# Second products of an expert step moved between the halves of the next step's up products

## The chip, the cores and the metric

One core of a Trainium2 chip runs the whole program. The metric is device time in microseconds, the median of several runs; lower is better. The profile and the trace come from one execution of their own.

## The reference, cut to what matters

The program is a two-layer encoder trunk over 272 tokens (256 and 16 meta tokens) of width 1024. The part that matters here is the channel mixer of the second layer: a router sends each token to two of eight experts, and each expert is a SwiGLU of width 3584.

```python
def swiglu(h, w_gate, w_up, w_down):
    return (jax.nn.silu(h @ w_gate) * (h @ w_up)) @ w_down

for e in range(N_EXPERTS):
    y = y + combine[..., e:e + 1] * swiglu(h, e_gate[e], e_up[e], e_down[e])
```

All weights are float32: 8 experts x 3 x 1024 x 3584, read once from HBM.

## The kernel before, in words

The experts are ordered by the number of their tokens. The five fullest are "big" (room for 128 rows), the last three "small" (room for 64). Each expert's width of 3584 is cut into seven slices of 512, so that there are 56 steps, 35 big and 21 small. `steps` is their order, fixed when the program is built: the first seven are big, then a small step stands behind every big one or every second one, and the last four are big.

A step has three products. The gate product `pg` and the up product `pu` (`project`, L1148) multiply the step's rows, as the stationary operand, with 512 columns of weights, over eight blocks `k` of 128 features. The second product, or down product (`down`, L1220), multiplies the flipped result of the step, `hh` and `hl` (`hs` for small ones), with 8 blocks of weights into `pyb0`, `pyb1` (or `pys0`, `pys1`), which add up over an expert's seven steps. The flip is done by transposes on TensorE and evictions (`flip_later`, L1190, big; `flip_small`, L1199, small; the latter also adds the two halves and applies the SiLU, in three further pieces of work that are put into `side`).

The order is written out by hand: in step i come the gate products (the flip of step i - 1 ahead of block k = 4), the up products, then the down products of step i - 1. Engines run their own instructions in this order.

A weight comes as a tile of 128 x 2048 float32 (`raw`, 1024 KB), loaded by SP's queue (L84); 15 such tiles fit. It has two units of 1024 columns, two blocks each. To be multiplied with float32's precision at a faster rate, a unit is split in two: ScalarE casts the high part `w_hi` (L104), VectorE subtracts to get the low part `w_lo` (L127). Four units are held in this split form (`W_BUFS`). Big rows are split as well, so a block takes three matmuls (high x high, high x low, low x high, L1159, L1163, L1165); small rows have high and low side by side in the 128 columns of the stationary operand, so a block takes two. One unit in four of the gate and up weights of a big step is "plain": it is multiplied as it is, in full float32, and needs no split.

`W.release` gives a unit back and issues the next cast, `W.lo` issues the subtraction, and `beside` (L1135) does both with one piece of `side` between them, after every second block. When both units of a tile are split or used, the next tile is loaded into its place. `keep_rows` (L1095) takes the sums of a finished expert to `y_rows` in HBM by ScalarE's queue; `fetched` brings the rows of the next expert by transposes in four pieces (`behind`).

Of the kernel before, what the change touches and what calls it, by code (L numbers as in the profile page):

```python
# [39 lines left out]
ALONE, IDS_AT, COUNT_AT, SUMS_FROM, QUIET = 6, 1, 2, 4, 3  # L40
PLAIN_AT = 6
BIG, CAP, SMALL_CAP = 5, 128, 64
LAST_AHEAD, LAST_FLIP, LAST_TABLE = 3, 3, (0, 2)
POOL_AFTER = (2, 4, 6, 7)

# [120 lines left out]
def body(tc, xT, w_pw1, w_pw2, w_gu, w_dn, w_pool, m_gate, m_up, m_down, small, moe_g,  # L166
# [34 lines left out]
    tiles = []  # L201
# [17 lines left out]
    steps = [(of_small if i in small_at else of_big).pop(0) for i in range(NE * FT)]  # L219
    expert_at = {}  # L220

    def tile_of(w, q, f, p):
        return w[expert_at[q], f, p] if q else w[0, f, p]

    def moe_tile(w, i):
        q, f = steps[i]
        for p in range(2):
            plain = (1,) if q < BIG and p and w is not m_down else ()
            tiles.append((lambda p=p: tile_of(w, q, f, p), [1024, 1024], plain))

    for i in range(len(steps)):
        moe_tile(m_gate, i)
        moe_tile(m_up, i)
        if i:
            moe_tile(m_down, i - 1)
    moe_tile(m_down, len(steps) - 1)
    W = Weights(nc, raw_pool, hi_pool, lo_pool, tiles)
    load_x(0)
    W.load(parts=[(256, lambda k=k: load_x(k)) for k in (2, 4, 6)] +
# [85 lines left out]
    def blocks(w, n):  # L325
        return [t.rearrange("p (k m) -> p k m", k=n) for t in w]
# [25 lines left out]
    def add_mean(ps, n, x):  # L352
        PE.matmul(ps, lhsT=mean, rhs=x, start=(n == 0), stop=(n == KC - 1))


    with ExitStack() as cs:
# [131 lines left out]
        def sums(lag=0):  # L488
            ready = [x for x in shifted if x[0] <= group_i - lag]
            del shifted[:len(ready)]  # L490
            for i, total in enumerate((mu, msq)):
                for _, c, sq in ready:
                    add_mean(total, n_sum[i], z(c) if i == 0 else sq)
                    n_sum[i] += 1

        pc, group_i = {}, 0
        while diags:
            group, t = diags.pop(0)
# [55 lines left out]
        for k in range(KC):  # L554
            normed(k + 1)
            centre(k + 2)
            s = u[:, k]
# [59 lines left out]
    with ExitStack() as cs:  # L617
# [53 lines left out]
        for s in range(2):  # L671
# [7 lines left out]
            for m in range(KC):  # L679
                ps = psum.tile([128, T], F32, name="mm")  # L680
# [8 lines left out]
                last = s == 1 and m == KC - 1  # L689
# [14 lines left out]
                if s == 1 and m in POOL_AFTER[:-1]:  # L704
                    i = POOL_AFTER.index(m)
# [51 lines left out]
    with ExitStack() as cs:  # L757
# [97 lines left out]
        for t in range(2):  # L855
            ps = pp[:, t * NE:t * NE + NE]
# [238 lines left out]
    def keep_rows(py, q, small):  # L1095

        to, n = own_rows[q % 2], SMALL_CAP if small else CAP
        start = (BIG - 1) * CAP + (q - BIG) * n if small else q * n

        def keep(s):  # L1100
            dst = to[:n, s * 512:(s + 1) * 512]
            ACT.copy(dst, py[s][:n])
            if small:
                DVE.tensor_add(dst, py[s][n:], dst)

        return [lambda: keep(0), lambda: keep(1), lambda: None,
                lambda: nc.scalar.dma_start(y_rows[start:start + n], to[:n])]
# [19 lines left out]
    with ExitStack() as cs:  # L1127
# [5 lines left out]
        side = []  # L1133

        def beside():  # L1135

            W.release()
            if side:
                side.pop(0)()
            W.lo()  # L1140
# [4 lines left out]
        def sums(of):  # L1145
            return [py_pool.tile([128, 512], F32, name="py%s%d" % (of, s)) for s in range(2)]

        def project(ps, x, small, mid=None, behind=()):  # L1148
            n = SMALL_CAP if small else CAP
            behind = list(behind)  # L1150
            for k in range(KC):
                i = k % 2
                if i == 0:
                    w = blocks(W.next(), 2)
                if k == 4 and mid:
                    mid()

                hi = x[k - i][:, i, :128]
                PE.matmul(ps, lhsT=hi, rhs=w[0][:, i], start=(k == 0),  # L1159
                          stop=(k == KC - 1 and len(w) == 1))  # L1160
                if len(w) > 1:
                    if not small:
                        PE.matmul(ps, lhsT=x[k - i][:, i, n:], rhs=w[0][:, i], start=False,  # L1163
                                  stop=False)
                    PE.matmul(ps, lhsT=hi, rhs=w[1][:, i], start=False, stop=(k == KC - 1))  # L1165
                if i and k < KC - 1:
                    beside()
                    if behind:
                        behind.pop(0)()
            return behind  # L1170

        def flip(h_t, tiles):
            n = 4 // len(tiles)
            for i, (hi, lo) in enumerate(tiles):
                ps = pm.tile([128, 512], F32, name="m")[:, :n * 128]
                for j in range(n):
                    PE.transpose(ps[:, j * 128:(j + 1) * 128],
                                 h_t[:, (i * n + j) * 128:(i * n + j + 1) * 128], ident)
                split(hi, lo, ps)
            return tiles  # L1180
# [9 lines left out]
        def flip_later(h_t):  # L1190

            ps = pm.tile([128, 512], F32, name="m")
            turned(ps, h_t)
            hi, lo = flip_tiles()[0]
            ACT.copy(hi, ps)
            side.insert(0, lambda: DVE.tensor_sub(lo, ps, hi.bitcast(F32)))
            return [(hi, lo)]

        def flip_small(gu):  # L1199


            n = SMALL_CAP
            v = ws.tile([128, 2, 4, n], F32, name="v", tag="yl", bufs=1)
            for a, t in enumerate(gu):
                ps = pm.tile([128, 512], F32, name="m")
                turned(ps, t)
                ps = ps.rearrange("p (j c) -> p j c", j=4)
                ACT.copy(v[:, a], ps[:, :, :n])
                DVE.tensor_add(v[:, a], ps[:, :, n:], v[:, a])
            t = ws.tile([128, 4, 2 * n], F32R, name="hs", tag="hh", bufs=1)  # L1210

            def through():
                DVE.tensor_mul(v[:, 0], v[:, 0], v[:, 1])
                ACT.copy(t[:, :, :n], v[:, 0])

            side[:0] = [lambda: ACT.activation(v[:, 0], v[:, 0], AF.Silu), through,
                        lambda: DVE.tensor_sub(t[:, :, n:], v[:, 0], t[:, :, :n].bitcast(F32))]
            return t

        def down(py, hT, small, f, mid=None):  # L1220
            for i in range(8):
                s, j = divmod(i, 4)
                if j % 2 == 0:
                    wh, wl = blocks(W.next(), 2)
                a, *b = [hT[:, j]] if small else flipped(hT, j)
                ps = py[s]
                first, last = f == 0 and j == 0, f == FT - 1 and j == 3
                PE.matmul(ps, lhsT=a, rhs=wh[:, j % 2], start=first, stop=False)  # L1228
                if b:
                    PE.matmul(ps, lhsT=b[0], rhs=wh[:, j % 2], start=False, stop=False)  # L1230
                PE.matmul(ps, lhsT=a, rhs=wl[:, j % 2], start=False, stop=last)  # L1231
                if j % 2:
                    if i == LAST_FLIP and mid:
                        mid()
                    beside()
# [90 lines left out]
        for q in range(1, NE):  # L1326
            e = experts[q] = Expert(q, ws, pm)
# [9 lines left out]
        prev, py_of, n_fetched = None, {}, 0  # L1337
# [4 lines left out]
        for n_step, (q, f) in enumerate(steps):  # L1342
            e = experts[q]
            last = n_step == len(steps) - 1
# [65 lines left out]
            behind = []  # L1410
            if n_step in after_of:
                new = experts[after_of[n_step]]
                behind = [lambda kk=kk, new=new: new.fetched(kk) for kk in range(0, KC, 2)]
            pg = pg_pool.tile([128, 512], F32, name="pg")
            hT = []

            def turn():
                if prev:
                    t, p = prev[0], prev[1]
                    hT.append(flip_small(t) if p.small else flip_later(t))  # L1420

            project(pg, e.x, e.small, turn)
            W.release()
            if e.small:
                ht = [ws.tile([128, 512], F32, name=n, bufs=1) for n in ("ht", "ut")]
                ACT.activation(ht[0], pg, AF.Copy, scale=e.r)
            else:
                ht = ws.tile([128, 512], F32, name="ht", bufs=1)
                ACT.activation(ht, pg, AF.Silu, scale=e.r)
            W.lo()  # L1430
            pu = pu_pool.tile([128, 512], F32, name="pu")
            behind = project(pu, e.x, e.small, None, behind)
            W.release()
            if e.small:
                ACT.activation(ht[1], pu, AF.Copy, scale=e.r)
# [4 lines left out]
                piece()  # L1440
            if prev:
                _, p, pf = prev
                if pf == 0:
                    py_of[p.of] = sums(p.of)
                py = py_of[p.of]
                if last:
                    last_T = [[t[:, i] for i in range(2)] for t in [
                        ws.tile([128, 2, 256], F32R, name="last_T", tag="x%db" % k, bufs=1)
                        for k in (0, 2)]]
                down(py, hT[0], p.small, pf, (lambda: flip(ht, last_T)) if last else None)  # L1450
                if pf == FT - 1:
                    side[:0] = keep_rows(py, p.q, p.small)
            prev = ht, e, f

        assert not side
# [27 lines left out]
        for s in range(2):  # L1483
            for j in range(0, 4, 2):
# [3 lines left out]
                x = [flipped(last_T, j + i) for i in range(2)]  # L1488
# [88 lines left out]
```

## Time and profile before

| | us |
|---|---|
| median of 3 runs | 1323.21 (1322.23 to 1323.44) |
| the profiled execution | 1321.8 |
| its span, first to last instruction | 1319.8 |
| of it the expert steps 7 to 54 | 495.40 to 1277.30 |

The granted TensorE clock is 0.993 over the span. The span is what the views of the trace cover; the device time of the same execution is 2.0 us longer. Times in views count from the start of the span.

### The profile page before, as it was taken

What the parts mean: (1) busy time and instruction counts of PE and PEld (TensorE: products, weight loads), DVE (VectorE), ACT (ScalarE), POOL (GpSimd) and SP (SyncE); (2) the same over time, 40 slices, a digit from 0 to 9 for tenths busy, and PEclk for the clock granted to TensorE, in tenths of its full rate; (3) what the DMA queues carried; (4) which work ended last, traced back from release to release, by engine and by line L of the source; (5) the groups of instructions that cost most, each with busy time, mean ns of one, the idle gap of its engine ahead of it and who ended that gap; (6) DMA issues with size and microseconds to landing.
All of it is one profiled execution on the core that took longest, in us unless ns stands there. A gap on an engine that the chain in (4) does not pass through costs nothing.

```text
span 1319.8 us, 19130 instructions
## 1 busy us (share of the span) xinstructions
PE 1281.9 (97%) x6655; PEld 1037.6 (79%) x6655; DVE 1099.2 (83%) x1471; ACT 928.5 (70%) x1263; POOL 21.8 (2%) x37
## 2 busy tenths in 40 slices
PE   9999999999989989999999999999999999999995
PEld 9989999999967767777777677777777777777773
DVE  7997885666677878999899888989988997999876
ACT  6765553445555657888788877888878887888764
POOL 0000000000010010000000000000000000000010
PEclk9999999999999999999999999999999999999998
DMA  9800436524868899999999599999999999799960
GB/s 365 312 2 1 147 129 223 191 82 161 337 218 306 309 349 347 422 422 414 384 407 392 226 419 422 419 422 420 374 417 374 422 421 421 316 422 421 411 273 35
DMA packets 61401, 414.22 MB, mean 314 GB/s; under 512 B 6896, under 2 KB 7536, under 8 KB 14320
## 3 DMA queue, kind: packets, MB, share of 16 engines
q1 hardware_dynamic: 58032, 402.22, 76.9%
q0 software_dynamic: 1872, 6.55, 1.4%
q10 hardware_dynamic: 1392, 4.14, 0.8%
q8 instruction: 54, 0.88, 0.3%
q14 instruction: 51, 0.42, 0.1%
HBM read 407.90 MB, written 4.98 MB: 313 GB/s over the span
## 4 chain that ended last, share of the span: by engine, by line
PE 85%; DVE 8%; issue 4%; ACT 1%; DMA 1%; DVEq 0%; ACTq 0%
PE pu L1159 10%; PE pg L1159 9%; PE mm L307 7%; PE mm L306 7%; PE mm L305 7%; PE pu L1165 6%; DVE w_lo L127 6%; PE pyb L1228 5%; PE pyb L1231 5%; PE pyb L1230 5%; PE pg L1165 5%; PE pg L1163 4%; PE mm L507 4%; PE pu L1163 3%; PE pys L1231 2%
## 5 line engine op out<-in xcount | busy, mean ns | idle before, releaser
L127 DVE TENSOR_TENSOR w_lo<-raw,w_hi 128x1024 fp32r<-128x1024 f32 (+1 forms) x704 | 820.5, 1203 | 138.5 <-ACT w_hi L104 132.9
L104 ACT CAST w_hi<-raw 128x1024 fp32r<-128x1024 f32 (+1 forms) x704 | 710.4, 1034 | 254.2 <-PE mm L306 70.9
L305 PE MATMUL mm<-xh,w_hi 128*128 128x272 f32 x480 | 139.9, 291 | 0.0
L307 PE MATMUL mm<-xh,w_lo 128*128 128x272 f32 x480 | 139.6, 291 | 0.0
L306 PE MATMUL mm<-xl,w_hi 128*128 128x272 f32 x480 | 139.0, 290 | 0.0
L1228 PE MATMUL pyb<-w_hi,hh 128*128 128x512 f32 x272 | 112.4, 413 | 0.0
L1231 PE MATMUL pyb<-w_lo,hh 128*128 128x512 f32 x272 | 107.5, 395 | 1.5 <-DVE w_lo L127 1.5
L1230 PE MATMUL pyb<-w_hi,hl 128*128 128x512 f32 x272 | 107.4, 395 | 0.0
L306 PEld LDWEIGHTS mm<-xl,w_hi 128*128 128x128 f32 x480 | 90.8, 189 | 0.6 <-DVE xl L322 0.2
L307 PEld LDWEIGHTS mm<-xh,w_lo 128*128 128x128 f32 x480 | 90.6, 189 | 0.6 <-DVE w_lo L127 0.2
L305 PEld LDWEIGHTS mm<-xh,w_hi 128*128 128x128 f32 x480 | 90.7, 189 | 0.1
L1228 PE MATMUL pys<-w_hi,hs 128*128 128x512 f32 x168 | 74.2, 441 | 0.0
L1159 PE MATMUL pu<-raw,x6b 128*128 128x512 f32 x140 | 67.8, 608 | 0.0
L1231 PE MATMUL pys<-w_lo,hs 128*128 128x512 f32 x168 | 66.3, 395 | 0.0
L1159 PE MATMUL pg<-raw,x6b 128*128 128x512 f32 x140 | 65.8, 592 | 0.0
L1231 PEld LDWEIGHTS pyb<-w_lo,hh 128*128 128x128 f32 x272 | 51.2, 188 | 15.8 <-DVE w_lo L127 2.0
L1230 PEld LDWEIGHTS pyb<-w_hi,hl 128*128 128x128 f32 x272 | 51.3, 189 | 13.6 <-issue 2.4
L1228 PEld LDWEIGHTS pyb<-w_hi,hh 128*128 128x128 f32 x272 | 51.2, 188 | 12.8 <-ACT w_hi L104 2.4
L401 DVE SCALAR_TENSOR_TENSOR v<-u,sm,v 128x271 f32<-128x271 f32 (+29 forms) x137 | 55.5, 484 | 0.0
L305 PE MATMUL mm<-gh,w_hi 128*128 128x272 f32 x176 | 50.7, 288 | 0.0
L307 PE MATMUL mm<-gh,w_lo 128*128 128x272 f32 x176 | 50.7, 288 | 0.0
L306 PE MATMUL mm<-gl,w_hi 128*128 128x272 f32 x176 | 50.5, 287 | 0.0
(405 smaller groups left out, 2352.6 us busy)
## 6 DMA issues: line engine op xcount, KB each, us to landing
raw<-m_gate SPq DMA_DIRECT2D x112, 1024.0 KB, 12.6
raw<-m_up SPq DMA_DIRECT2D x112, 1024.0 KB, 11.8
raw<-m_down SPq DMA_DIRECT2D x111, 1024.0 KB, 12.0
raw<-w_gu SPq DMA_DIRECT2D x22, 1024.0 KB, 4.9
raw<-w_dn SPq DMA_DIRECT2D x16, 704.0 KB, 4.1
raw<-w_pw SPq DMA_DIRECT2D x10, 1024.0 KB, 17.5
y_rows<-rows ACTq DMA_DIRECT2D x4, 512.0 KB, 2.8
h<-xT SPq DMA_DIRECT2D x4, 272.0 KB, 4.5
```

Of the source, the lines that this page charges most:

```text
L104: self.nc.scalar.copy(hi[:, :n], self.raw[i][:, s:s + n])
L127: self.nc.vector.tensor_sub(lo, self.raw[i][:, s:s + n], hi.bitcast(F32))
L305: PE.matmul(ps, lhsT=w[0], rhs=x[0], start=first, stop=False)
L306: PE.matmul(ps, lhsT=w[0], rhs=x[1], start=False, stop=False)
L307: PE.matmul(ps, lhsT=w[1], rhs=x[0], start=False, stop=last)
L401: DVE.scalar_tensor_tensor(v[:, c, j:], u[:, c, :T - j], w, v[:, c, j:], op0=OP.mult, op1=OP.add)
L1159: PE.matmul(ps, lhsT=hi, rhs=w[0][:, i], start=(k == 0), stop=(k == KC - 1 and len(w) == 1))
L1163: PE.matmul(ps, lhsT=x[k - i][:, i, n:], rhs=w[0][:, i], start=False, stop=False)
L1165: PE.matmul(ps, lhsT=hi, rhs=w[1][:, i], start=False, stop=(k == KC - 1))
L1228: PE.matmul(ps, lhsT=a, rhs=wh[:, j % 2], start=first, stop=False)
L1230: PE.matmul(ps, lhsT=b[0], rhs=wh[:, j % 2], start=False, stop=False)
L1231: PE.matmul(ps, lhsT=a, rhs=wl[:, j % 2], start=False, stop=last)
```

## The change

In the steps 1 to 54 the down products of the step before are cut in two halves of four blocks. The first half comes ahead of block k = 4 of the up products, the second behind the up products. The tiles are loaded in the new order of use: gate 0, gate 1, up 0, down 0, up 1, down 1. The last step keeps the old order. The flip of a small step's result is done ahead of block k = 2 of the next gate products, not k = 4; that of a big one stays at k = 4.

```diff
+TURN_AT = {False: 4, True: 2}
...
-    for i in range(len(steps)):
-        moe_tile(m_gate, i)
-        moe_tile(m_up, i)
-        if i:
-            moe_tile(m_down, i - 1)
-    moe_tile(m_down, len(steps) - 1)
+    for i in range(len(steps)):
+        woven = 0 < i < len(steps) - 1
         for p in range(2):
+            moe_tile(m_gate, i, p)
+        for p in range(2):
+            moe_tile(m_up, i, p)
+            if woven:
+                moe_tile(m_down, i - 1, p)
+        if i and not woven:
+            for p in range(2):
+                moe_tile(m_down, i - 1, p)
+    for p in range(2):
+        moe_tile(m_down, len(steps) - 1, p)
...
-        def project(ps, x, small, mid=None, behind=()):
+        def project(ps, x, small, between={}, behind=()):
...
+                if k in between:
+                    between[k]()
                 if i == 0:
                     w = blocks(W.next(), 2)
-                if k == 4 and mid:
-                    mid()
...
-        def down(py, hT, small, f, mid=None):
-            for i in range(8):
+        def down(py, hT, small, f, halves=(0, 1), mid=None):
+            for i in range(4 * halves[0], 4 * halves[-1] + 4):
...
             def turn():
-                if prev:
-                    t, p = prev[0], prev[1]
-                    hT.append(flip_small(t) if p.small else flip_later(t))
-
-            project(pg, e.x, e.small, turn)
+                t, p, _ = prev
+                hT.append(flip_small(t) if p.small else flip_later(t))
+
+            def weave(s):
+                _, p, pf = prev
+                if s == 0 and pf == 0:
+                    py_of[p.of] = sums(p.of)
+                down(py_of[p.of], hT[0], p.small, pf, (s,))
+
+            project(pg, e.x, e.small, {TURN_AT[prev[1].small]: turn} if prev else {})
...
-            behind = project(pu, e.x, e.small, None, behind)
+            woven = prev and not last
+            behind = project(pu, e.x, e.small, {4: lambda: weave(0)} if woven else {}, behind)
...
-                if last:
+                if woven:
+                    weave(1)
+                else:
+                    py = py_of[p.of]
...
-                down(py, hT[0], p.small, pf, (lambda: flip(ht, last_T)) if last else None)
+                    down(py, hT[0], p.small, pf, mid=lambda: flip(ht, last_T))
                 if pf == FT - 1:
-                    side[:0] = keep_rows(py, p.q, p.small)
+                    side[:0] = keep_rows(py_of[p.of], p.q, p.small)
```

## Rows read from the trace of the kernel before

**Rows 1.** The page, busy time by engine, whole span
```profile
PE 1281.9 (97%) x6655; PEld 1037.6 (79%) x6655; DVE 1099.2 (83%) x1471; ACT 928.5 (70%) x1263; POOL 21.8 (2%) x37
```

**Rows 2.** Windows of the 21 small steps: bounds, length, busy us by engine, clock, DMA
```profile
716.99:733.79 16.80, 15.37 (x69) 11.47 (x68) 16.21 (x19) 14.38 (x21) 1.19 (x1) 1.00 1.02 410
...
861.54:876.05 14.51, 13.98 (x61) 10.63 (x60) 14.51 (x14) 13.52 (x17) 0.00 (x0) 1.00 1.01 422
...
972.96:989.12 16.16, 15.39 (x70) 11.41 (x69) 15.39 (x18) 14.28 (x20) 0.00 (x0) 1.00 1.01 420
1005.50:1021.49 15.99, 14.51 (x62) 10.56 (x60) 15.93 (x16) 14.60 (x19) 0.00 (x0) 1.00 0.84 323
...
1118.43:1132.28 13.85, 13.85 (x61) 10.75 (x60) 13.69 (x13) 13.20 (x16) 0.00 (x0) 1.00 1.01 422
...
1210.47:1225.27 14.80, 14.27 (x61) 10.57 (x60) 14.80 (x14) 13.82 (x17) 0.00 (x0) 1.00 1.02 422
sum 309.39, PE 297.27 PEld 225.32 DVE 307.23 ACT 286.89 POOL 1.19; mean PE 14.16 PEld 10.73 DVE 14.63 ACT 13.66 POOL 0.06
```

**Rows 3.** Windows of big steps, one behind a small step
```profile
845.14:861.54 16.40, 16.40 (x69) 12.14 (x68) 13.50 (x16) 11.95 (x15) 0.00 (x0) 1.00 1.01 420
```

**Rows 4.** Timeline of TensorE in a small step: start, length, instruction, idle before
```profile
861.54 0.39 PE L1159 MATMUL pg<-w_hi,x0s 128*128 128x512 f32 x1
...
863.40 0.60 PE L1188 MATMUL m<-iw,ht 128*128 128x128 f32 x4
...
867.60 0.40 PE L1159 MATMUL pu<-w_hi,x4s 128*128 128x512 f32 x1
868.53 0.50 PE L1165 MATMUL pu<-w_lo,x4s 128*128 128x512 f32 x1 [0.53 <-DVE w_lo L127]
```

**Rows 5.** The chain of waits through a big step: start, length, piece
```profile
848.10 0.87 PE m L1188 x8
...
850.37 1.72 PE pg L1159 x4
...
857.99 0.23 PE pys L1228
```

**Rows 6.** Waits, 500 to 1280 us: waiter, releaser, us in total, times, longest
```profile
PE pu L1165 <- DVE w_lo L127: 9.9, 19, 0.7
...
PE m L1019 <- DVE x0s L1024: 2.2, 2, 1.4
...
ACT w_hi L104 <- DMA raw<-m_up: 0.7, 2, 0.4
```

**Rows 7.** Timeline of VectorE, 848 to 880 us
```profile
855.57 0.42 DVE L1217 TENSOR_TENSOR hs<-v,hs 128x256 fp32r<-128x256 f32 x1
...
859.84 6.90 DVE L127 TENSOR_TENSOR w_lo<-raw,w_hi 128x1024 fp32r<-128x1024 f32 x6 [0.75 <-ACT w_hi L104]
866.66 0.68 DVE L1196 TENSOR_TENSOR hl<-m,hh 128x512 fp32r<-128x512 f32 x1
867.26 13.86 DVE L127 TENSOR_TENSOR w_lo<-raw,w_hi 128x1024 fp32r<-128x1024 f32 x12
```

**Rows 8.** Timeline of ScalarE, two stretches
```profile
858.76 5.79 ACT L104 CAST w_hi<-raw 128x1024 fp32r<-128x1024 f32 x6 [1.59 <-PE pys L1228]
...
766.12 1.05 ACT L104 CAST w_hi<-raw 128x1024 fp32r<-128x1024 f32 x1 [0.35 <-PE pyb L1230]
```

**Rows 9.** DMA view, 860 to 890 us
```profile
DMA packets 1735, 12.64 MB, mean 421 GB/s; under 512 B 193, under 2 KB 193, under 8 KB 193
```

**Rows 10.** Waits of SP's queue, 500 to 1280 us
```profile
SPq L84 <- DMA y_rows<-rows: 100.7, 7, 22.5
```

**Rows 11.** Timeline of SP's queue around the longest stop
```profile
725.10 2.80 SPq L84 DMA_DIRECT2D raw<-m_gate  x2
750.63 1.25 SPq L84 DMA_DIRECT2D raw<-m_up  x2
```

**Rows 12.** The loads issued from 750 to 752 us
```profile
DMA to landing us min/median/max: 5.0/6.2/7.3
```

More of the change, by code (lines that the diff above doesn't have):

```diff
@@ L223, in tile_of, with moe_tile @@
         return w[expert_at[q], f, p] if q else w[0, f, p]
-    def moe_tile(w, i):
+    def moe_tile(w, i, p):
         q, f = steps[i]
+        plain = (1,) if q < BIG and p and w is not m_down else ()
+        tiles.append((lambda: tile_of(w, q, f, p), [1024, 1024], plain))
+    for i in range(len(steps)):
+        woven = 0 < i < len(steps) - 1
         for p in range(2):
-            plain = (1,) if q < BIG and p and w is not m_down else ()
-            tiles.append((lambda p=p: tile_of(w, q, f, p), [1024, 1024], plain))
-    for i in range(len(steps)):
-        moe_tile(m_gate, i)
-        moe_tile(m_up, i)
-        if i:
-            moe_tile(m_down, i - 1)
-    moe_tile(m_down, len(steps) - 1)
+            moe_tile(m_gate, i, p)
[8 more added lines that the diff above has]
+        moe_tile(m_down, len(steps) - 1, p)
     W = Weights(nc, raw_pool, hi_pool, lo_pool, tiles)
@@ L1442, in body @@
                 _, p, pf = prev
-                if pf == 0:
-                    py_of[p.of] = sums(p.of)
-                py = py_of[p.of]
-                if last:
+                if woven:
+                    weave(1)
+                else:
+                    py = py_of[p.of]
                     last_T = [[t[:, i] for i in range(2)] for t in [
```

## Prediction

> **What bounds the kernel now.** The page shows TensorE busy for 97% of the span [rows 1], which says little, since matmuls overlap in it. So I went on to windows by step. A step is one 512-column slice of one expert; 35 steps are big (128 rows, three matmuls for each block of 128 features) and 21 small (64 rows, two). The windows of the 21 small steps [rows 2] last 309.39 us together, and not equally: four take about 13.86 us (one shown), twelve about 14.52 (one shown), one 14.80, two about 15.98 (one shown), two 16.80 and 16.16. In the 14.51 us row VectorE is busy for all of it. A big step behind a small one takes 16.40 us [rows 3], with TensorE busy throughout and VectorE for 13.50.
>
> The timeline of TensorE [rows 4] gives the price of a matmul with 512 columns: eight from 861.54 to 863.40, 0.2325 us each. Eight transposes take 0.87 [rows 5], so four cost 0.44. A small step behind a big one has 16 + 16 + 24 matmuls: 56 x 0.2325 + 0.44 = 13.46 us without a wait. The ordinary small step is 1.05 us above that. Where it goes: the up product at 867.60 is followed only at 868.53 by the next, which waited for the low part of a weight. The list of waits [rows 6] has this line 19 times. Why: in the timeline of VectorE [rows 7] low parts come at (6.90 - 1.23)/5 = 1.135 us each, while a small product uses up a unit (four matmuls) in 0.93. The casts on ScalarE come faster, 5.79 us for six [rows 8]. So the second products of a small expert, then the gate and up products of the next small step, make twelve fast units in a row, and the four units that are ready ahead don't last.
>
> The pair of a big and a small step leaves room: VectorE is busy 13.50 + 14.51 = 28.0 us of 30.91 [rows 2, 3]. It is the order that makes the wait, not the sum.
>
> **The change, part by part.** No matmul, cast or transfer is added or removed. *Second products between the halves of the up products.* The unit order of a small step becomes: four gate units, two up, two down (big, 24/4 matmuls = 1.40 us per unit), two up, two down. The big step before it ends with two up units (one of them half plain) and two fast down units. The longest fast run is then 2 + 4 + 2 = 8 units instead of 12.
>
> I make the ledger from the moment D at which TensorE begins the last fast units before a small step. Today that is all four units of a small second product, at 857.99 [rows 5]; VectorE starts the first missing low part at 859.84, D + 1.85 [rows 7]. Ready times are then 3.08 for the first, 1.135 later for each of the next three, and 0.60 more where the low part of the flipped tile sits between (866.66 to 867.26). First the check on today's order: the third up unit is needed at D + 9.99 and ready at 10.5, a wait of 0.5, the fourth at 0.2 more: 0.72 us, against 1.05 measured. The other 0.33 are small bumps, as an answer that comes just in time still costs about 0.1 us each. Now the new order, need less ready: third gate unit 4.40 - 3.08 = 1.32 us to spare, fourth 1.12, first up 0.91, second 0.71; flipped tile 8.12 - 7.07 = 1.05; first down 8.36 - 8.22 = 0.14; second 0.38; third up 0.39; fourth 0.18; third down 0.20; fourth 0.44. Nothing is late, and three are close, so I charge three bumps, 0.3 us: an ordinary small step takes 13.76 us and saves 0.75. Ends: 1.05 with no bump, 0.55 with 0.5 us of them.
>
> The sum for the 21: twelve ordinary x 0.75 = 9.0. Four that follow two big ones, 0.40 above the floor today, x 0.2 = 0.8 (0 to 0.4). The 14.80 one: 1.0. The two at 15.98 come one step after a small expert's rows are added up on VectorE, two more operations of 0.62 before the down units: the ledger goes negative by 0.54 and again by 0.61, so 13.46 + 1.15 + 0.2 = 14.8, and 2 x 1.15 = 2.3 is saved. The two with fetched rows waited 2.2 us together for x0s [rows 6]; the third pair of transposes now comes behind two down units, 2.8 us later, so that wait goes, and 0.3 each of the ordinary one: 2.8. Together 15.9 us. The first seven steps keep their waits, which come of the router's work: 0, between -2 and +2.
>
> *Flip of small experts one unit earlier.* It costs nothing on its own: the transposes are the same, and the second products now need their left operand 8.2 us after the flip starts (0.87 for eight transposes, then 1.40 + 1.40, a unit of two plain blocks 1.72 [rows 5], two up units 2.80), where the chain today takes 855.57 + 0.42 - 848.10 = 7.9 us from the first transpose to the end of VectorE's last operation on it [rows 5, 7]. The cover is 0.3 us if the chain keeps its length; it should shorten, as the two operations beside it now fall one unit sooner.
>
> *Order of loads.* The same tiles in the order of use. A pair needs 12 tiles of 1024 KB, 12.58 MB; the transfers run at 421 GB/s [rows 9], so 29.9 us. The new pair is 16.40 + 13.76 = 30.16: just above it, no new bound. The Trainium skill, "DMA: Bandwidth & Descriptors", section "Where 436 GB/s comes from", says that from HBM about 358 GB/s per core bind; by that a pair would need an estimated 35.1 us and the change could bring nothing. The trace disagrees, with 421 GB/s held for the 30 us stretch.
>
> What transfers can still do is arrive late. SP's queue stops seven times for the write of a finished expert's rows [rows 10]; in the worst it issues nothing from 727.9 to 750.63 [rows 11]. The tile issued then lands 5.0 us later [rows 12], and its first cast, counted in order of use, is at 766.12 [rows 8]: 10.5 us to spare, the least that I found. Up to there I collect about 1 x 0.2 + 4 x 0.75 + 0.2 + 1.7 = 5 us, so even with all landings unmoved 5 us stay. The waits for loads in the expert part are 0.7 us in all [rows 6].
>
> The profiled execution took 1321.8 us (span 1319.8 plus 2.0); 1321.8 - 15.9 = 1305.9. The median of the runs is 1.4 above it, so I forecast 1307.
>
> **The rivals.** (1) *The wait moves to the second products.* For it: the ledger leaves 0.14 to 0.20 us at three places, and VectorE fills the small step. If each were late by some 0.2 us, the small steps save 0.35 instead of 0.75: 12 x 0.35 + 0 + 0.5 + 1.5 + 2 = 8, so 1315. Against it: today's check came out low only by bumps, which are in. (2) *Transfers become the bound.* Gained time eats the cushion while the stops of SP stay; if a stop grew by the 10.5 us cushion, some 6 to 8 us would be lost again: 1314. Against: SP's stops begin and end with the compute steps. Were the transfers already at their limit with today's pair (12.58 MB in 30.91 us, 407 GB/s), nothing would change, 1323; the 421 GB/s of [rows 9] leave that 1 in 100. This is what the skill's page on DMA bandwidth, above, would come to. (3) *Slower: the small flip's result comes too late.* Its place is the first second-product matmul in the 21 steps that follow a small one, now needed 0.3 us after today's chain would end. If the queue order on VectorE puts it one unit further back (1.15 us) it is 0.85 late; 21 x 0.76 us = 15.9 eats the gain, and from 0.88 on the kernel is slower by over 0.2%; at two units back, 2.0 us, 21 x 2.0 - 16 = 26 us, 1349. Against: VectorE idles in the big step today. (4) *Nothing happens*, because VectorE's sum binds after all: 1323; the 28.0 of 30.9 us [rows 2, 3] speak against.
>
> **How the numbers follow.** Forecast 66%: its own range 1300 to 1312 (12 x 1.05 + 1.6 + 1.3 + 5 + 4 = 24.5 saved at most, about 1299; 12 x 0.55 + 0 + 0.6 + 1.2 + 1.5 = 9.9 at least, 1313). Rival 1 15%, rival 2 7%, rival 3 8%, rival 4 4%. The range 1300 to 1316 takes in rivals 1 and 2 and leaves out 2 in 10: rival 3, rival 4 and the tails. A change within 0.2% (2.6 us) is about what a measurement of this kernel can't tell from none. Faster 0.87 (forecast, 1, 2), same 0.05 (4 and a little of 3), slower 0.08.
>
> **What would show it.** Right: small steps of 13.6 to 13.9 us, big ones still 16.40, the wait of up products for low parts nearly gone, no new line of waits on the flipped tile hs, casts still not waiting for loads. Wrong: a wait of the pys products for hs or of pyb for w_lo in each pair, big steps above 16.5, or casts that wait for raw tiles after one of SP's stops.

## The result and the profile after

| | before | after |
|---|---|---|
| median | 1322.72 us (4 runs, 1320.91 to 1323.44) | 1301.26 us (4 runs, 1300.72 to 1302.38) |
| the profiled execution | 1321.8 | 1302.38 |
| its span | 1319.8 | 1300.2 |

After to before is 0.9845, with a 95% interval from 0.9833 to 0.9857: 1.5% faster. The forecast was 1307.

The page answers to [rows 1]: TensorE's share rises from 97% to 98%, and each engine runs as many instructions as before, in a shorter span.

```profile
PE 1272.4 (98%) x6655; PEld 1038.2 (80%) x6655; DVE 1096.6 (84%) x1471; ACT 927.5 (71%) x1263; POOL 22.4 (2%) x37
```

The windows of the small steps after, with the columns of [rows 2] (bounds, length, busy us of each engine, clock, DMA): first one with fetched rows, one that adds up rows, an ordinary one, one behind two big ones, the one that took 14.80, and the sum of all 21.

```profile
710.64:725.94 15.30, 15.30 (x69) 11.41 (x68) 15.18 (x18) 14.19 (x21) 1.73 (x1) 1.00 1.00 417
742.33:757.41 15.08, 14.12 (x62) 10.71 (x60) 14.90 (x15) 14.30 (x19) 0.00 (x0) 1.00 1.01 411
...
851.51:865.13 13.62, 13.62 (x61) 10.84 (x60) 13.51 (x13) 13.24 (x17) 0.00 (x0) 1.00 1.02 423
...
1102.19:1115.64 13.45, 13.45 (x61) 10.91 (x60) 13.28 (x13) 13.22 (x16) 0.00 (x0) 1.00 1.01 422
...
1192.10:1205.71 13.61, 13.61 (x61) 10.86 (x60) 13.49 (x13) 13.23 (x17) 0.00 (x0) 1.00 1.01 421
sum 291.67, PE 289.75 PEld 228.87 DVE 288.81 ACT 281.92 POOL 1.73; mean PE 13.80 PEld 10.90 DVE 13.75 ACT 13.42 POOL 0.08
```

The sum fell from 309.39 to 291.67, by 17.7 us. The ordinary step stands at 13.62, 0.16 above the 13.46 of its matmuls. The big step behind a small one is where it was in [rows 3], 16.39 against 16.40:

```profile
835.12:851.51 16.39, 16.39 (x70) 12.12 (x68) 14.35 (x16) 12.14 (x16) 0.00 (x0) 1.00 1.01 419
```

The list of all waits of TensorE from 480 to 1260 us answers to [rows 6], where the low part of a weight stopped an up product 19 times and the fetched rows stopped it twice:

```profile
PE pu L1173 <- DVE w_lo L128: 1.1, 2, 0.5
PE pyb L1239 <- DVE w_lo L128: 0.8, 2, 0.4
```

The stretch that the table of before names steps 7 to 54 (steps count from 0, and it begins with step 6, which took 18.73 us and takes 18.69) went from 781.90 us to 764.24. Ahead of it, steps 0 to 5, with a few matmuls that stand before them, gave another 2.4 us, of which nothing was forecast:

```profile
374.26:493.50 119.24, 112.26 (x465) 81.64 (x464) 91.03 (x167) 69.98 (x82) 3.41 (x4) 0.97 0.82 306
493.50:1257.74 764.24, 762.32 (x3241) 578.94 (x3240) 689.68 (x699) 627.64 (x753) 10.15 (x9) 1.00 0.98 404
```

The first of these windows in the kernel before:

```profile
373.72:495.40 121.68, 113.91 (x464) 82.87 (x464) 91.18 (x167) 69.95 (x82) 4.04 (x4) 0.96 0.83 305
```

17.7 and 2.4 are 20.1; the steps begin 0.5 later, which leaves the 19.6 by which the spans differ.

### The profile page after: what moved, and what is told of

Same layout as the page of the kernel before. It is cut to its first block, busy times and chain, and to the rows that moved or that the text cites. A ratio compares the mean times of both kernels' runs of the same rounds, so it can differ in the third digit from the quotient of the medians.

```text
span 1300.2 us, 19132 instructions
## 1 busy us (share of the span) xinstructions
PE 1272.4 (98%) x6655; PEld 1038.2 (80%) x6655; DVE 1096.6 (84%) x1471; ACT 927.5 (71%) x1263; POOL 22.4 (2%) x37
## 4 chain that ended last, share of the span: by engine, by line
PE 91%; DVE 3%; DMA 3%; ACT 1%; issue 1%; SPq 0%; ACTq 0%; DVEq 0%
PE pu L1167 11%; PE pg L1167 10%; PE mm L315 7%; PE mm L313 7%; PE mm L314 7%; PE pg L1173 6%; PE pu L1173 6%; PE pyb L1239 5%; PE pyb L1236 5%; PE pyb L1238 5%; PE mm L515 4%; PE pg L1171 4%; PE pu L1171 3%; PE pys L1236 3%; PE pys L1239 3%; PE m L1196 2%
```

## The experiments

My theory is that of the forecast: the wait came of the number of fast units in a row against the units that stand ready, and shortening the row removes it. A fast unit is one that TensorE uses up in 0.93 us, sooner than the 1.135 us in which VectorE makes a low part. The weave is the new place of the second products, between and behind the halves of the next up products. The rivals are that the earlier flip, the order of loads or the first steps did it, and that something else is now the bound. Each edit below is against the changed kernel unless it says otherwise. Each ratio is that of the means to runs of the kernel before that were made alongside (their medians are 1321.68 to 1324.37 us), with its 95% interval.

**The flip left at block 4** (e1_flip_at_4):

```diff
-TURN_AT = {False: 4, True: 2}
+TURN_AT = {False: 4, True: 4}
```

> The changed kernel with the flip of small steps put back to block k = 4, everything else woven. My theory: the flip one unit earlier is not a gain by itself, but what the weave needs. In the queue of VectorE the last operation on hs then stands behind the low part of the third up unit, ready some 10.7 us after the start of a big step, while TensorE wants hs at 9.6: a wait of about 1.1 us in each of the 21 big steps behind a small one. Big steps 17.3 to 17.6 us instead of 16.4, in all +20 us (15 to 27): about 1322, the whole gain gone. Rival: the chain from the transposes to hs takes only the 6.4 us that it takes in the changed kernel, and starting 2.8 us into the step it would still be done at 9.2: no wait, 1301 to 1303.

Measured: 1333.23 us, ratio to before 1.0064 (1.0036 to 1.0092), slower than before. The direction is the theory's, the price is larger. The list of waits, and the windows of a small step and of the big step behind it:

```profile
PE pys L1236 <- DVE hs L1225: 24.1, 21, 1.2
```
```profile
833.71:847.33 13.62, 13.62 (x62) 10.85 (x60) 13.51 (x13) 13.23 (x17) 0.00 (x0) 1.00 1.01 420
847.33:865.13 17.80, 16.64 (x69) 12.06 (x68) 14.43 (x16) 12.13 (x16) 0.00 (x0) 1.00 1.01 421
```

The small steps keep their 13.62, and the 21 big steps behind them pay 17.80 instead of 16.39: 1.41 x 21 = 29.6 us. The timeline of VectorE in this run says why:

```profile
854.56 0.42 DVE L1221 TENSOR_TENSOR v<-v 128x256 f32<-128x256 f32 x1
856.58 1.23 DVE L128 TENSOR_TENSOR w_lo<-raw,w_hi 128x1024 fp32r<-128x1024 f32 x1 [1.60 <-ACT w_hi L105]
857.73 0.42 DVE L1225 TENSOR_TENSOR hs<-v,hs 128x256 fp32r<-128x256 f32 x1
```

The last operation on the flipped tile, `hs`, stands in VectorE's queue behind the low part of a weight, and that one waits 1.60 us for its cast. The transposes began at 850.11, so the chain takes 857.73 + 0.42 - 850.11 = 8.04 us. The last up product starts at 856.65, so without the wait the second products would have begun 0.23 us later, at 856.88, 6.8 us after the transposes; they begin at 858.20. In the changed kernel the same queue reads:

```profile
841.06 0.42 DVE L1221 TENSOR_TENSOR v<-v 128x256 f32<-128x256 f32 x1
841.40 1.22 DVE L128 TENSOR_TENSOR w_lo<-raw,w_hi 128x1024 fp32r<-128x1024 f32 x1
842.53 0.42 DVE L1225 TENSOR_TENSOR hs<-v,hs 128x256 fp32r<-128x256 f32 x1
844.38 1.23 DVE L128 TENSOR_TENSOR w_lo<-raw,w_hi 128x1024 fp32r<-128x1024 f32 x1 [1.43 <-ACT w_hi L105]
```

One unit earlier, the low part that must wait for its cast (1.43 us) has come to stand behind `hs` and no longer ahead of it. The transposes begin at 836.51, `hs` is done at 842.95, after 6.4 us, and its first matmul comes at 844.68: 1.7 us to spare.

**The earlier flip alone, in the kernel before** (e2_flip_only), against before:

```diff
-        def project(ps, x, small, mid=None, behind=()):
+        def project(ps, x, small, mid=None, behind=(), mid_at=4):
...
-                if k == 4 and mid:
+                if k == mid_at and mid:
...
-            project(pg, e.x, e.small, turn)
+            project(pg, e.x, e.small, turn, mid_at=2 if prev and prev[1].small else 4)
```

> The kernel before with the flip of small steps one unit earlier, nothing woven. My theory: no change, 1322 to 1324, small steps still 14.5 us, since hs isn't waited for there and the wait of the up products for low parts stays. Rival: the earlier flip moves VectorE's two additions away from the fast run and brings part of the gain: 1315 or less.

Measured: 1323.15 us, ratio 0.9998 (0.9970 to 1.0025). No change by itself, within 0.3%, as expected; e1_flip_at_4 shows that the weave needs it.

**The weave in small steps only, and in big steps only** (e3_in_small, e4_in_big):

```diff
-        woven = 0 < i < len(steps) - 1
+        woven = 0 < i < len(steps) - 1 and steps[i][0] >= BIG
...
-            woven = prev and not last
+            woven = prev and not last and e.small
...
```

(the other with `< BIG` and `not e.small`; a step that isn't woven does both halves behind its up products.)

> Woven only in small steps (the second products of a big step between the halves of a small step's up products); big steps keep the old order. The longest run of fast units is 4 + 4 + 2 = 10 instead of 8 (changed) or 12 (before). By the ledger the first down unit's low part is 0.28 us late and two places are just in time: small steps behind a big-after-small one 14.1 us (before 14.52, changed 13.62), those behind two big ones 13.5. With the first seven steps (all big, so not woven) back at the time of before: about 1312 (1308 to 1315). Rival: the load order or the flips make the gain, not the run length: at either kernel's time, 1301 or 1322.

> Woven only in big steps; small steps keep the old order. The longest run of fast units is 2 + 4 + 4 = 10. By the ledger the third and fourth up units' low parts are 0.1 to 0.2 us late: ordinary small steps about 14.05 us, those behind two big ones still 13.86 as before. The first seven steps as in the changed kernel. About 1311 (1307 to 1314). Rival as for the weave in small steps alone: 1301 or 1322.

Measured: 1310.91 us, ratio 0.9887 (0.9855 to 0.9920), and 1311.62, ratio 0.9890 (0.9858 to 0.9923), both as expected. An ordinary small step, in the windows of the first and of the second run:

```profile
824.23:838.28 14.05, 13.75 (x62) 10.80 (x61) 14.05 (x14) 13.41 (x17) 0.00 (x0) 1.00 1.01 420
```
```profile
824.51:838.57 14.06, 13.93 (x61) 10.75 (x60) 13.94 (x13) 13.35 (x17) 0.00 (x0) 1.00 1.01 420
```

Either half alone leaves ten fast units in a row, once as four second-product, four gate and two up units, once as two, four and four. Above 13.46 us, twelve in a row cost 1.05, ten cost 0.60 in both runs, and eight cost 0.16: some 0.22 us for each unit, near the 1.135 - 0.93 = 0.20 by which a low part is slower than its use. The half that is cut doesn't matter, the length does.

**A fifth unit in split form, in the kernel before and in the changed one** (e5_five_before, e6_five_after):

```diff
-RAW, RAW_BUFS, MORE_RAW = 2048, 10, (3, 2)
-UNIT, W_BUFS = 1024, 4
+RAW, RAW_BUFS, MORE_RAW = 2048, 9, (3, 2)
+UNIT, W_BUFS = 1024, 5
...
-        self.raw, self.home, self.done, self.ahead = {}, {}, {}, W_BUFS
+        self.raw, self.home, self.done, self.ahead = {}, {}, {}, 4
...
+            if n_step == ALONE:
+                W.ahead = W_BUFS
```

> The kernel before, not woven, with five units held in split form instead of four from the seventh step on, and nine raw tiles in the first pool instead of ten to make room. My theory: what makes the wait is how long the fast run is against the units ready ahead, so one unit more does what four fast units fewer do. By the ledger the third up unit is then ready at D + 9.35 and needed at 9.97: small steps 13.5 to 13.7 us in the old order, about 1305 (1302 to 1309). Rival: the gain comes from the order of the products or of the loads as such, or VectorE's sum binds: 1320 to 1324.

> The changed kernel with five split units from the seventh step on and nine raw tiles in the first pool. My theory: what is left of the waits goes too: 0.16 us in each of 13 steps, about 1.3 in each of the two steps in which a small expert's rows are added up. About 1297 (1295 to 1299), against 1301 of the changed kernel. Rival: what is left are not waits for low parts, or the raw tile that is missing is felt: 1300 to 1303.

Measured: 1309.98 us, ratio 0.9913 (0.9888 to 0.9937), and 1300.8 (1298.1 to 1307.32), ratio 0.9846 (0.9806 to 0.9886): both longer than the theory said. The place that it speaks of came out as it said, and another one broke. The windows of e5_five_before, an ordinary small step in the old order, and step 5:

```profile
830.54:844.03 13.49, 13.49 (x61) 10.94 (x60) 13.49 (x13) 13.22 (x17) 0.00 (x0) 1.00 1.01 420
468.69:501.74 33.05, 22.19 (x81) 15.37 (x80) 16.46 (x19) 12.53 (x17) 4.30 (x2) 0.79 0.78 284
```

The old order with one more unit ahead has no waits in ordinary small steps. But step 5 takes 33.05 us, 9.3 more than before, and 28.85 instead of 21.61 in e6_five_after. (An earlier line of the program raises the number of units to `W_BUFS`, so that five were in use from the first steps on.)

**A small expert's rows added up eight pieces later** (e7_keep_later):

```diff
-        return [lambda: keep(0), lambda: keep(1), lambda: None,
+        return [lambda: None] * (8 if small else 0) + [lambda: keep(0), lambda: keep(1), lambda: None,
```

> The changed kernel with the rows of a finished small expert added up eight pieces later, behind the small step's second products instead of in its gate products. My theory: the two steps of 15.06 us go to 13.7, and nothing else moves: about 1298.5 (1297 to 1300). Rival: the write of the rows, which SP's queue stops for, comes some 10 us later with them, SP's stops grow, and loads land late: 1300 to 1306.

Measured: 1299.52 us (1298.14 to 1299.81), ratio to before 0.9834 (0.9816 to 0.9852); the median is 1.7 us below that of the changed kernel. The two steps that the ledger had singled out fall from 15.08 and 15.05 to the ordinary length:

```profile
740.99:754.61 13.62, 13.62 (x62) 10.86 (x61) 13.50 (x13) 13.25 (x17) 0.00 (x0) 1.00 1.01 424
...
989.12:1002.75 13.63, 13.63 (x61) 10.87 (x60) 13.51 (x13) 13.24 (x17) 0.00 (x0) 1.00 1.02 421
```

**Eleven raw tiles instead of fifteen** (e8_six_raw), `RAW_BUFS` 10 to 6:

> The changed kernel with six raw tiles in the first pool instead of ten (eleven in all instead of fifteen): some 10 us of cushion less, as much as the least spare time that a tile had after one of SP's stops. Theory that transfers are near to being the bound: tiles land late after each of the stops in the expert steps, casts wait for loads for some us in all, 1305 to 1315. Rival, which I hold for likelier: SP is stopped since it is far ahead of the write that it waits for; with fewer tiles it is less far ahead, the stops get shorter by as much, and the time stays within 1301 to 1303.

Measured: 1301.66 us, ratio 0.9856 (0.9834 to 0.9879), the time of the changed kernel; the rival was right. The line of SP's stops for the rows that are written, in the changed kernel and then in this run:

```profile
SPq L85 <- DMA y_rows<-rows: 103.8, 7, 18.8
```
```profile
SPq L85 <- DMA y_rows<-rows: 52.2, 7, 9.7
```

With fewer tiles SP runs less far ahead, and its stops are half as long. Arrival of loads is no bound here, nor near one.

**The weave from step 7 on only** (e9_from_7):

```diff
-        woven = 0 < i < len(steps) - 1
+        woven = ALONE < i < len(steps) - 1
...
-            woven = prev and not last
+            woven = prev and not last and n_step > ALONE
...
```

> The changed kernel, but with the second products woven between the up products only from step 7 on; the first seven steps keep the old order. Theory: the 2.4 us that the changed kernel gained in the steps 1 to 6 come of the weave, which lets step 5 meet VectorE's burst of router work better; without it these steps take 121.7 us as before and the median is 1303.7 (1302.5 to 1305). Rival: they come of something else or of chance from run to run, and the median stays at 1301.3 (1300.5 to 1302.3).

Measured: 1306.41 us (1302.62 to 1307.89), ratio 0.9859 (0.9829 to 0.9888), above the range of the theory. In the profiled execution (1305.03) steps 0 to 5 take 122.0 us, about as before the change, and the 21 small ones 291.7, as after it. That the 122.0 comes so near to 121.7 is in part luck: steps 0 and 1 are 1.1 us shorter than before the change, and step 5 is 1.4 longer. But step 5 says the same in every trace. It takes 21.61 or 21.62 us in the five kernels that have four units and the weave in the first steps (the changed one, e1, e4, e7, e8), and 23.24 to 25.16 in the four without the weave there (before, e2, e3, e9). So most of the 2.4 us belongs to the weave in step 5, and there to one wait and what followed it. The timeline of TensorE before, and windows of 2 us (the clock is the third figure from the end):

```profile
471.85 0.39 PE L1163 MATMUL pg<-w_hi,x0b 128*128 128x512 f32 x1
474.56 0.50 PE L1165 MATMUL pg<-w_lo,x0b 128*128 128x512 f32 x1 [2.32 <-DVE w_lo L127]
...
476.54 0.63 PE L1163 MATMUL pg<-w_hi,x2b 128*128 128x512 f32 x1
```
```profile
474.00:476.00 2.00, 1.44 (x4) 1.21 (x5) 2.00 (x3) 0.07 (x1) 1.30 (x1) 0.74 1.01 422
476.00:478.00 2.00, 2.00 (x6) 1.52 (x6) 2.00 (x3) 0.97 (x1) 0.00 (x0) 0.50 0.99 393
```

And the same in the changed kernel:

```profile
474.20 0.50 PE L1173 MATMUL pg<-w_lo,x0b 128*128 128x512 f32 x1 [1.69 <-DVE w_lo L128]
474.54 0.39 PE L1167 MATMUL pg<-w_hi,x0b 128*128 128x512 f32 x1
```
```profile
474.00:476.00 2.00, 1.79 (x8) 1.49 (x9) 2.00 (x4) 0.80 (x1) 0.94 (x1) 1.00 0.92 354
```

Before, TensorE waits 2.32 us and then works at a granted clock of 0.50, its lower level of 1.2 GHz: matmuls come every 0.43 us, not every 0.2325, from about 474.9 to 478.25, which costs some 1.6 us. After, it waits 1.69 and the clock stays at 1.00. That is 0.6 + 1.6 of the 2.2 us by which step 5 is shorter. Only the 0.6 came with the order in every trace: that matmul waits 2.32 us in the four kernels without the weave there, and 1.66 to 1.69 in the five with it. Behind the shorter wait the clock stayed at 1.00 in all five, and behind 2.32 us it fell in three of the four. In e3_in_small it did not fall:

```profile
473.76 0.50 PE L1173 MATMUL pg<-w_lo,x0b 128*128 128x512 f32 x1 [2.32 <-DVE w_lo L128]
```
```profile
474.00:476.00 2.00, 2.00 (x10) 1.60 (x10) 2.00 (x3) 1.05 (x1) 0.50 (x1) 1.00 0.98 412
476.00:478.00 2.00, 2.00 (x12) 1.67 (x11) 2.00 (x2) 1.55 (x3) 0.00 (x0) 1.00 1.01 354
```

So the half clock is not bound to this wait. In e3 the rest of step 5's excess is a wait of 0.9 us for the first small expert's fetched rows; e9 has one of 1.4 us beside the half clock, which neither theory had. Why e9's median lies 2.7 us above the forecast isn't settled.

**Five units from step 7 on, with the later rows, and the same number in the kernel before** (e10_five_keep; e11_five_before_7 is the same without the later rows, against before). Beside the first three changed lines of e5 and the line of e7:

```diff
-                W.ahead = W_BUFS
+                W.ahead = 4
...
+            if n_step == ALONE + 1:
+                W.ahead = W_BUFS
```

> The changed kernel, with a small expert's rows added up eight pieces later, and with five units in split form instead of four from step 7 on; up to there four, and one raw tile fewer throughout. Theory: what the weave leaves (0.16 us in each ordinary small step) is lookahead that a fifth unit gives, and the late landing of the first small expert's rows in the earlier runs with five units came of having them before step 7. So ordinary small steps 13.46, the two that add up rows 13.5, the first seven steps 118.6 to 119.3: 286.4 us for the 21 instead of 291.7, median 1296.5 (1295 to 1298). Rival: the fifth unit, which reaches further into the raw tiles, or the tile that it costs, still delays the first small expert's rows, and the median is 1300 to 1303.

> The kernel before, old order and old flip, with five units in split form from step 7 on (four up to there, one raw tile fewer throughout). Theory: the wait that the change removes is a shortage of lookahead, so that a fifth unit alone removes it: the 21 small steps take 291.7 us as with five units throughout, the first seven steps 121.7 as before, median 1305 (1303.5 to 1306.5). Rival: the first seven steps suffer as they did with five units throughout, and the median is 1310.

Measured: 1303.5 us (1298.24 to 1309.45), ratio 0.9840 (0.9805 to 0.9876), and 1309.33 (1302.09 to 1315.89), ratio 0.9880 (0.9846 to 0.9915). The rival came nearer in both (in e10_five_keep the median lies 0.5 us above its range). The small steps are as the theory said (286.4 and 291.5 us for the 21), and step 5 again is not, at 33.62 and 31.80. The timeline of TensorE in e10_five_keep, the wait and what follows it:

```profile
488.36 0.44 PE L1027 MATMUL m<-iw,rows 64*128 64x64 f32 x2 [11.83 <-DMA rows<-x_rows,at]
488.74 0.79 PE L1167 MATMUL pu<-w_hi,x2b 128*128 128x512 f32 x1
489.33 0.63 PE L1171 MATMUL pu<-w_hi,x2b 128*128 128x512 f32 x1
```

The rows of the first small expert are fetched by an indirect load in step 5, and here they come 11.8 us late, with the half clock behind. The DMA view from 462 to 478 us gives the time from issue to landing, in the changed kernel and then in e10_five_keep:

```profile
rows<-x_rows,at POOLq DMA_INDIRECT x2, 5.7
```
```profile
rows<-x_rows,at POOLq DMA_INDIRECT x2, 14.1
```

**The fifth buffers as a pool of their own, first used in step 7, with the later rows** (e12_fifth_late); `RAW_BUFS` 9, `W_BUFS` 4, `W.ahead` 5 from step 7 on, and in `hi`:

```diff
+                pools = self.hi_pool, self.lo_pool
+                if self.ahead == W_BUFS + 1:
+                    if self.since % self.ahead == 0:
+                        pools = self.fifth
+                    self.since += 1
```

> As the run before with five units and the later adding up of a small expert's rows, but the fifth buffer pair is a pool of its own that is first used in step 7; up to there four buffers turn over as in the changed kernel. Theory: in the earlier runs with five units the fifth buffer itself, though its use was meant to begin at step 7, let the casts run one unit further ahead from the start, which brought step 5 forward by about 3 us into a time in which the rows of the first small expert land late (a wait of 10 to 12 us for their indirect load). Kept out of the first steps, it costs nothing there: they take 118.6 to 119.4 us, the 21 small steps 286.4, and the median is 1296.3 (1295 to 1298). Rival: it is the raw tile that was given up, or chance in that load; then step 5 still takes 28 to 33 us and the median is 1300 to 1304.

Measured: 1299.41 us (1297.21 to 1309.05), ratio 0.9827 (0.9789 to 0.9866); the median is above the theory's range. The windows of the steps 4 and 5 in e10_five_keep, and then here:

```profile
450.83:468.65 17.82, 17.82 (x74) 13.21 (x72) 17.43 (x34) 11.45 (x13) 1.08 (x2) 1.00 0.93 352
468.65:502.27 33.62, 21.79 (x81) 15.08 (x80) 16.61 (x20) 12.32 (x17) 5.61 (x2) 0.80 0.75 255
```
```profile
449.20:468.54 19.34, 18.08 (x73) 13.13 (x72) 15.71 (x27) 11.67 (x13) 1.08 (x2) 1.00 0.84 313
468.54:493.27 24.73, 21.42 (x81) 14.48 (x80) 18.23 (x27) 12.52 (x17) 2.34 (x2) 0.93 0.95 351
```

With the same raw tile given up, step 4 keeps the length that it has in the changed kernel, 19.4, and step 5 loses 9 of its extra 12 us. So the tile alone doesn't make step 5 as long as it is in e10_five_keep; what these two kernels differ by is the fifth buffer in the first steps. But the theory's "brought step 5 forward" is wrong: step 5 begins at 468.54 here and at 468.65 there. What differs is the traffic ahead of it. Windows of 4 us in e10_five_keep, and then here, with the share of the DMA engines in the column before the last:

```profile
464.00:468.00 4.00, 4.00 (x16) 2.61 (x15) 3.66 (x17) 1.83 (x2) 0.00 (x0) 1.00 0.97 359
```
```profile
464.00:468.00 4.00, 2.74 (x11) 1.76 (x10) 3.86 (x10) 0.89 (x1) 0.53 (x1) 1.00 0.51 207
```

In e10_five_keep SP issues the two gate tiles at 464.24, here at 467.22, and a lull in the transfers is filled with weights. The indirect load follows a write of the rows that it reads; here POOL waits 3.2 us between the two, there 8.0, though the write was issued sooner (at 465.21 and at 462.24).

The three kernels without a lull are alike (e5, e10 and e11, where no 4 us from 460 to 472 us are under 270 GB/s): POOL waits 8.0 to 9.5 us, and TensorE then 10.5 to 11.8 us for the load. But e6_five_after, which has the five buffers too, keeps a lull (114 GB/s from 464 to 468 us) and POOL waits 3.6 us, and still its load takes 10.2 us and TensorE waits 4.1. So the filled lull is not all of it, and why the indirect load itself takes 14.1 us isn't settled; with four buffers it took from 5.7 us (changed kernel) to 10.8 (e9_from_7).

The rest of step 5's excess in e12_fifth_late is a wait of 1.6 us for the same load and the half clock after it. In the profiled execution (1297.21) the 21 small steps take 286.6 us, 5.1 less than after the change. But the six runs of this kernel spread over 12 us, with a lower mean clock in the long ones (0.985 in that of 1309.05), and its median is that of e7_keep_later. Those of e10_five_keep spread as far (1298.24 to 1309.45), and each kernel has one trace, so chance in that load, the other half of the rival, isn't excluded. The long runs left no trace; that they wait longer for that load is not shown.

The best versions, e7_keep_later and e12_fifth_late, stand 1.7 and 1.9 us below the changed kernel by their medians. Every run of the first lies below every run of the changed kernel (1299.81 against 1300.72), but the intervals of the ratios overlap.

## Why the prediction was right, and by how much it was off

**What bounds it: right.** Two of the experiments undo the cause from either side. Ten fast units in a row instead of eight bring some 0.44 us back to each ordinary small step, and a fifth unit ahead removes the wait without any reordering.

**The terms of the sum**, forecast and measured, in us:

| term | forecast | measured |
|---|---|---|
| twelve ordinary small steps | 9.0 | 12 x (14.52 - 13.62) = 10.8 |
| four behind two big ones | 0.8 | 4 x (13.86 - 13.46) = 1.6 |
| the 14.80 one | 1.0 | 1.2 |
| two that add up rows | 2.3 | 1.8 |
| two with fetched rows | 2.8 | 2.3 |
| the first seven steps | 0 | 2.4 |
| sum | 15.9 | 20.1 |

The step that was mis-sized most is "The first seven steps keep their waits": one of them shortened by 0.6 us, and the clock no longer fell behind it. The 1.6 us that the clock gave are no gain to count on, since it stayed up behind the longer wait too in e3_in_small. Next are the bumps, the small costs of an answer that comes just in time: "I charge three bumps, 0.3 us". One of the three places has a bump, the one where the ledger left the least, 0.14 us. The timelines of TensorE and of VectorE in an ordinary small step, which answer to [rows 4] and [rows 7], show it on the first low part of the second products:

```profile
857.53 0.39 PE L1236 MATMUL pyb<-w_hi,hh 128*128 128x512 f32 x1
857.75 0.40 PE L1238 MATMUL pyb<-w_hi,hl 128*128 128x512 f32 x1
858.04 0.50 PE L1239 MATMUL pyb<-w_lo,hh 128*128 128x512 f32 x1
858.38 0.39 PE L1236 MATMUL pyb<-w_hi,hh 128*128 128x512 f32 x1
```
```profile
856.77 1.22 DVE L128 TENSOR_TENSOR w_lo<-raw,w_hi 128x1024 fp32r<-128x1024 f32 x1
```

From 857.75 to 858.38 two matmuls take 0.63 us and not 0.465: 0.16, the whole of 13.62 - 13.46. There was nothing to spare at this place: the low part ends at 856.77 + 1.22 = 857.99, and its matmul could have started at 857.98. The ledger's 0.14 came of its start. It counts from D = 857.99, read in the chain of waits, but the 16 matmuls of 0.2325 us ahead of 861.54 begin at 857.82. So VectorE starts 2.02 us behind D and not 1.85, all the ledger's spare times are 0.17 too large, and its check on the old order comes to 0.89 of the 1.05 us instead of 0.72. The changed kernel has nearly the same lag: eight matmuls ahead of 851.51 begin at 849.65, and VectorE starts at 851.62, 1.97 later. The later places gain the 0.16 that is lost here; in this trace each has 0.24 us or more to spare and costs nothing. The steps behind two big ones reach the floor, so all of their 0.40 went.

The two steps that add up rows stand 1.6 above the floor where the ledger said 1.35. VectorE's next operation follows each of the two 0.62 us after its start, as forecast (744.83 to 745.45, 746.58 to 747.19), but some 0.2 us of gaps come with them: the low part of the flipped tile begins 6.00 us behind the step's first low part (742.44 to 748.44), and 4.55 in an ordinary step (851.62 to 856.17). That is 1.45 us, and e7_keep_later, where these steps take 13.62 and 13.63, shows that it is all that sets them apart.

Of the 5.7 us between forecast and median, 3.5 lie in the profiled execution (1302.4 against 1305.9); the rest is that the median stood 1.1 us above the profiled execution in the forecast and stands 1.1 below it after. That rest, and the 1.6 us of the clock, are differences from one execution to the next of which the forecast has no term.

**Flip of small experts: "costs nothing on its own" held** (e2_flip_only), and so did the sign of its cover, but not its size. Forecast was 0.3 us to spare; measured are 1.7, since the chain shortened to 6.4 us, from 8.05 in the same view. (The forecast's 7.9 counts from 848.10 in the chain of waits; the timeline has the first transposes of the kernel before at 847.94.) I named the shortening and gave it no number. Rival 3 is real where the flip stays: e1_flip_at_4 is that rival on the chip, with 1.41 us a step, above the 0.88 from which it decides.

**Loads: no new bound, as forecast.** The DMA view of the changed kernel from 860 to 890 us, which answers to [rows 9]:

```profile
DMA packets 1731, 12.62 MB, mean 421 GB/s; under 512 B 192, under 2 KB 192, under 8 KB 192
```

Casts wait 0.5 us in all for loads, once, against 0.7 in [rows 6]. The rule of the Trainium skill by which the change could bring nothing ("DMA: Bandwidth & Descriptors", section "Where 436 GB/s comes from", about 358 GB/s per core from HBM) doesn't hold in this trace, with one core at work and 421 GB/s. Rivals 1 and 4 don't occur: beyond the bump, second products wait for low parts twice, 0.8 us in all.

## What to carry to other kernels

Where a slower engine prepares what a faster one uses in bursts, write a ledger of ready and needed times through the longest burst. Cutting the burst and deepening the lookahead were worth about the same in the small steps here (13.62 and 13.49 us), and the ledger said how much of either is enough. Take all its times from one view: a start read in another made every spare time 0.17 us too large. When work is moved ahead, look at what stands in front of its inputs in the other engines' queues: here one move that brings nothing alone decides between 21 us gained and 9 lost. And before giving a prefetch more room, look for small transfers on which a step depends: in e10_five_keep an indirect load landed after 14.1 us and not 5.7, and TensorE waited 11.8 us for it, where the small steps had gained 5.3 us (286.4 for the 21 and not 291.7).

## What the runs showed of the hardware that was not expected

A wait of TensorE can cost nearly as much again behind it. Behind 2.32 us the granted clock was 0.50 for some 3.3 us, which added 1.6 us; behind 1.69 us, at the same instruction, it stayed at 1.00; behind 11.83 us matmuls came every 0.43 us from 489.33 to about 493. The length of the wait alone doesn't decide: behind 1.61 us in step 5 of e12_fifth_late the clock fell to 0.50 (from 482 to 484 us), which added some 1.5 us (24.73 - 21.61 - 1.61), and behind 2.32 us in e3_in_small it stayed at 1.00.

SP's stops for the written rows depend on how far SP has run ahead: with eleven tiles instead of fifteen they fell from 103.8 to 52.2 us, at the same time of the kernel.
